# A 2x2x2 average pool: five 32 KB input buffers and a 32 KB first load in place of one 160 KB ring with a 64 KB first load

## The chip, the cores and the metric

The kernel runs on one core of a Trainium2 chip. Input and output lie in HBM, the chip's large memory; the work is done on tiles in SBUF, a memory of 128 partitions. The metric is the device time of one execution in microseconds (us). The kernel before takes 93.12 us, the median of three runs that lie between 93.12 and 93.19 us.

Three parts of the core matter here. SP (the sync engine) does no arithmetic: it issues every transfer of this kernel, one after the other, and can hold each issue back until a semaphore has a value. The 16 DMA engines carry the transfers. DVE (the vector engine) does all the additions. TensorE, ScalarE and, but for four constants that nothing here uses, GpSimd have no work.

## The reference

The input `x` is a float32 array of shape (8, 32, 32, 32, 32): batch, channels, depth, height, width. Every non-overlapping 2x2x2 block of depth, height and width is replaced by its mean:

```python
    out_d = d // kernel_size      # kernel_size is 2
    ...
    for i in range(out_d):
        for j in range(out_h):
            for k in range(out_w):
                ...
                window = x[:, :, d_s:d_s + kernel_size, h_s:h_s + kernel_size, w_s:w_s + kernel_size].copy()
                result[:, :, i, j, k] = np.mean(window, axis=(-3, -2, -1))
```

That is 33.55 MB to read and 4.19 MB to write, with seven additions and one multiplication for each output.

## The kernel before

Batch and channels together give 256 images, one to a partition: two tiles `t` of 128 partitions. An image is 32768 floats in a row, 128 KB. The kernel counts it in pieces of `KF` = 256 floats (1 KB): an image has 128 pieces, and 32 pieces are eight depth planes, 32 KB a partition, 4 MB over all partitions.

`plan` (line 42) lists the loads as (tile, first piece, pieces, place in the ring). The ring is a single SBUF tile of 160 pieces a partition. There are eight loads: one of 64 pieces (8 MB), five of 32 (4 MB) and at the end two of 16 (2 MB). The first four fill the ring exactly; the later four are written over parts that DVE has finished with.

`pool_unit` adds up what has landed, 32 pieces at a time or 16 for the two last loads, in place. Line 59 adds neighbouring depth planes, line 63 neighbouring columns, and line 66 neighbouring rows, multiplies by 0.125 and writes the result to one of two output tiles, `obuf`, one for each `t`. Line 66 also writes a sum to `dummy` that nobody reads; it shows in the profile as a short second instruction (DVE_READ_ACCUMULATOR2_ANT). Such a set of instructions is called a unit below: there are seven units of 32 pieces and two of 16.

Three stores on line 82 bring the results out: the whole first tile (2 MB, after the last unit of `t` = 0), 14/16 of the second (1.75 MB, after all its units but the last) and the last 2/16 (256 KB, after the last unit). They are written behind all loads in the program, and SP issues in the program's order: a transfer held back holds back all behind it. All transfers go through one hardware queue, in which each DMA engine takes its packets in order.

A framework derives the waits: a load into a part of the ring that was used before waits for the load that was there and for DVE's last instruction on it, a unit waits for its load, and a store for its units. At the end (line 92) SP waits for all transfers, two semaphores in one instruction, and all engines meet in a barrier. There is another barrier at the start, in a block ahead of the kernel's own. After compiling, the kernel takes the first load out of its own block and puts it into that opening block, ahead of SP's part of the barrier (its Drain instruction), so that the load leaves while the engines still meet. In the opening block as the kernel sees it at that point, SP's instructions begin with six that set registers (five moves and one that loads a base address); in the kernel before they stand ahead of the load.

Of the kernel before, what the change touches and what calls it, by code (L numbers as in the profile page):

```python
# [1 line left out]

# [4 lines left out]

F32 = mybir.dt.float32
KF = 256


@with_exitstack
def pool_rows(
    ctx: ExitStack,
    tc: tile.TileContext,
    x: bass.AP,
    kernel_size: int,
    out: bass.AP,
):
    nc = tc.nc  # L20
    assert kernel_size == 2, "only kernel_size == 2 supported"

    B, C, D, H, W = x.shape
    P = nc.NUM_PARTITIONS
    assert (B * C, D, H, W) == (2 * P, 32, 32, 32)
    add = mybir.AluOpType.add

    xv = x.rearrange("b c d h w -> (b c) (d h w)")  # L30
    ov = out.rearrange("b c d h w -> (b c) (d h w)")

    pool = ctx.enter_context(tc.tile_pool(name="ring", bufs=1))
    ring = pool.tile([P, 160 * KF], F32, name="ring")
    obuf = [pool.tile([P, 16 * KF], F32, name=f"obuf{t}") for t in range(2)]
    dummy = pool.tile([P, 1], F32, name="dummy")  # L40


    plan = [
        (0, 0, 64, 0),
        (0, 64, 32, 64),
        (0, 96, 32, 96),
        (1, 0, 32, 128),
        (1, 32, 32, 0),
        (1, 64, 32, 32),
        (1, 96, 16, 64),  # L50
        (1, 112, 16, 80),
    ]

    def pool_unit(buf, t, k0, kb):

        od = kb // 8
        a = buf.rearrange("p (o dd e) -> p o dd e", o=od, dd=2)
        b = buf[:, :od * 1024]
        nc.vector.tensor_add(  # L59
            out=b.rearrange("p (o e) -> p o e", o=od), in0=a[:, :, 0], in1=a[:, :, 1])  # L60
        bv = b.rearrange("p (e ww) -> p e ww", ww=2)
        c = buf[:, od * 1024:od * 1536]
        nc.vector.tensor_add(out=c, in0=bv[:, :, 0], in1=bv[:, :, 1])  # L63
        cv = c.rearrange("p (j hh k) -> p j hh k", hh=2, k=16)
        o0 = k0 * KF // 8
        nc.vector.tensor_tensor_reduce(  # L66
            out=obuf[t][:, o0:o0 + od * 256].rearrange("p (j k) -> p j k", k=16),
            in0=cv[:, :, 0], in1=cv[:, :, 1],
            scale=0.125, scalar=0.0, op0=add, op1=add, accum_out=dummy[:, :],
        )  # L70

    for t, k0, kb, r0 in plan:
        nc.sync.dma_start(
            out=ring[:, r0 * KF:(r0 + kb) * KF],
            in_=xv[t * P:(t + 1) * P, k0 * KF:(k0 + kb) * KF])
        for o in range(0, kb, 32):
            n = min(kb, 32)
            pool_unit(ring[:, (r0 + o) * KF:(r0 + o + n) * KF], t, k0 + o, n)


    for t, k0, kb in [(0, 0, 16), (1, 0, 14), (1, 14, 2)]:
        nc.sync.dma_start(
            out=ov[t * P:(t + 1) * P, k0 * KF:(k0 + kb) * KF],
            in_=obuf[t][:, k0 * KF:(k0 + kb) * KF],
        )


def kernel(tc: tile.TileContext, x: bass.AP, kernel_size: int, out: bass.AP):
    nc = tc.nc
    pool_rows(tc, x, kernel_size, out)  # L90
    tc.close()
    tc.compile()  # L92
    blocks = nc.main_func.blocks

    opening, program = blocks[0].instructions, blocks[tc.starting_block_idx].instructions
    load = next(i for i in program if isinstance(i, mybir.InstDMACopy))
    assert load.engine == nc.sync.engine
    barrier = next(  # L100
        n for n, i in enumerate(opening)
        if i.engine == load.engine and isinstance(i, mybir.InstDrain))
    program.remove(load)
    opening.insert(barrier, load)


# [1 line left out]
_INS = ['x', 'kernel_size']  # L108
_OUTS = [((8, 32, 16, 16, 16), 'float32')]

_NUMBERS = {'kernel_size': 2}


# [26 lines left out]
```

## Time and profile before

| what | value |
|---|---|
| median of three runs | 93.12 us |
| the profiled execution, its own time | 93.12 us |
| its span, first to last instruction | 91.3 us |
| DVE busy | 62.8 us, 69% of the span |
| DVE idle ahead of line 59, waiting for loads | 23.4 us, 22.0 us of it at the start |
| moved by DMA | 37.75 MB, mean 413 GB/s over the span |

The span begins with SP's first load at 0.00 us, and all times in the text count from there. 1.8 us of the execution's time lie outside of the span. A time "to landing" of a transfer counts from SP's issue until its last semaphore arrives, so issue and time to landing add up to the moment at which the data are there. SPq is SP's stream of issues and waits. The DMA share of a window counts each packet in the window in which it begins, so a short window can be well off; windows of several microseconds can be read.

### The profile page before, as it was taken

The page shows a single profiled execution, that of the slowest core. Times are in us where ns is not written, and L with a number is a line of the kernel's source. Part 1 is how long each engine was busy: PE and PEld are TensorE (multiplying, and loading weights), DVE is VectorE, ACT ScalarE, POOL GpSimd, SP SyncE. Part 2 cuts the span into 40 slices and gives each one's busy share as a digit, 9 for nine tenths or more (in the row PEclk, how much of TensorE's full clock was granted, in tenths as well). Part 3 has the DMA queues.
Part 4 walks back from the last instruction along what each step waited for, and adds up shares of the span by engine and source line. Part 5 has one row for each costly group of instructions (what it writes and reads, how often), then busy time and mean ns, then how long its engine had stood idle before and what let it go on. Part 6 is the DMA issues. An engine that isn't in the chain of part 4 may idle for free.

```text
span 91.3 us, 95 instructions
## 1 busy us (share of the span) xinstructions
DVE 62.8 (69%) x36; POOL 0.2 (0%) x4
## 2 busy tenths in 40 slices
DVE  0000000003999999999999999999993999999900
POOL 0000000000000000000000000000000000000000
DMA  9977799999999899999998899999997999899992
GB/s 459 430 344 344 316 402 459 459 459 459 445 402 416 373 430 459 459 459 459 445 402 387 387 445 459 459 459 459 416 416 337 438 431 445 309 423 445 410 413 109
DMA packets 1584, 37.75 MB, mean 413 GB/s; under 512 B 176, under 2 KB 176, under 8 KB 304
## 3 DMA queue, kind: packets, MB, share of 16 engines
q1 hardware_dynamic: 1584, 37.75, 97.4%
HBM read 33.55 MB, written 4.19 MB: 413 GB/s over the span
## 4 chain that ended last, share of the span: by engine, by line
DMA 55%; DVE 39%; issue 0%; DVEq 0%
DMA ring<-in_x_dram 55%; DVE ring L59 24%; DVE ring L63 10%; DVE obuf L66 5%; DVE dummy L66 0%; DVEq L92 0%
## 5 line engine op out<-in xcount | busy, mean ns | idle before, releaser
L59 DVE TENSOR_TENSOR ring<-ring 128x4096 f32<-128x4096 f32 (+1 forms) x9 | 35.4, 3946 | 23.4 <-DMA ring<-in_x_dram 23.4
L63 DVE TENSOR_TENSOR ring<-ring 128x2048 f32<-128x2048 f32 (+1 forms) x9 | 18.4, 2051 | 0.2
L66 DVE CUSTOM_DVE_ANT_1 obuf<-ring 128x1024 f32<-128x1024 f32 (+1 forms) x9 | 9.9, 1103 | 0.2
L66 DVE DVE_READ_ACCUMULATOR2_ANT dummy<- 128x1 f32 x9 | 0.7, 81 | 0.0
L121 POOL MEMSET const-uint8-127<- 128x1 uint8 x1 | 0.1, 103 | 0.0
L121 POOL MEMSET const-bfloat16-1.0<- 128x1 bf16 x1 | 0.1, 102 | 0.0
L121 POOL MEMSET const-float32-1.0<- 128x1 f32 x1 | 0.1, 99 | 0.0
L121 POOL MEMSET const-float32-0.0<- 128x1 f32 x1 | 0.1, 98 | 0.2 <-issue 0.2
## 6 DMA issues: line engine op xcount, KB each, us to landing
ring<-in_x_dram SPq DMA_DIRECT2D x5, 4096.0 KB, 30.8
ring<-in_x_dram SPq DMA_DIRECT2D x2, 2048.0 KB, 33.4
out_dram<-obuf SPq DMA_DIRECT2D x1, 2048.0 KB, 32.4
out_dram<-obuf SPq DMA_DIRECT2D x1, 1792.0 KB, 7.4
out_dram<-obuf SPq DMA_DIRECT2D x1, 256.0 KB, 3.8
ring<-in_x_dram SPq DMA_DIRECT2D x1, 21.9
```

Source lines behind the costliest of these rows:

```text
L59: nc.vector.tensor_add(out=b.rearrange("p (o e) -> p o e", o=od), in0=a[:, :, 0], in1=a[:, :, 1])
L63: nc.vector.tensor_add(out=c, in0=bv[:, :, 0], in1=bv[:, :, 1])
L66: nc.vector.tensor_tensor_reduce(out=obuf[t][:, o0:o0 + od * 256].rearrange("p (j k) -> p j k", k=16), in0=cv[:, :, 0], in1=cv[:, :, 1], s ...
L121: nc = _bacc.Bacc("TRN2", target_bir_lowering=False, num_devices=1)
```

## The change

The ring becomes a pool of five buffers of 32 pieces, of the same 160 KB together. The plan now lists eight buffers' contents, each loaded in one transfer of 32 pieces, or in two of 16 for the last two. So there are ten loads in place of eight: six of 32 pieces and four of 16. The former first load of 64 pieces is two loads of 32, and the load of `t` = 1 from piece 64 on, formerly 32 pieces, is two of 16. DVE does six units of 32 pieces and four of 16. The stores are the same three, with the same conditions. The first load is no longer put ahead of SP's Drain but ahead of SP's first instruction of the opening block.

```diff
-    pool = ctx.enter_context(tc.tile_pool(name="ring", bufs=1))
-    ring = pool.tile([P, 160 * KF], F32, name="ring")
-    obuf = [pool.tile([P, 16 * KF], F32, name=f"obuf{t}") for t in range(2)]
-    dummy = pool.tile([P, 1], F32, name="dummy")
+    pool_in = ctx.enter_context(tc.tile_pool(name="pin", bufs=5))
+    pool_out = ctx.enter_context(tc.tile_pool(name="pout", bufs=1))
+    obuf = [pool_out.tile([P, 16 * KF], F32, name=f"obuf{t}") for t in range(2)]
+    dummy = pool_out.tile([P, 1], F32, name="dummy")
...
     plan = [
-        (0, 0, 64, 0),
-        (0, 64, 32, 64),
-        (0, 96, 32, 96),
-        (1, 0, 32, 128),
-        (1, 32, 32, 0),
-        (1, 64, 32, 32),
-        (1, 96, 16, 64),
-        (1, 112, 16, 80),
+        (0, 0, (32,)),
+        (0, 32, (32,)),
+        (0, 64, (32,)),
+        (0, 96, (32,)),
+        (1, 0, (32,)),
+        (1, 32, (32,)),
+        (1, 64, (16, 16)),
+        (1, 96, (16, 16)),
     ]
...
-    for t, k0, kb, r0 in plan:
-        nc.sync.dma_start(
-            out=ring[:, r0 * KF:(r0 + kb) * KF],
-            in_=xv[t * P:(t + 1) * P, k0 * KF:(k0 + kb) * KF])
-        for o in range(0, kb, 32):
-            n = min(kb, 32)
-            pool_unit(ring[:, (r0 + o) * KF:(r0 + o + n) * KF], t, k0 + o, n)
+    for t, k0, parts in plan:
+        tin = pool_in.tile([P, 32 * KF], F32, tag="tin", name="tin")
+        views = []
+        o = 0
+        for kb in parts:
+            v = tin[:, o * KF:(o + kb) * KF]
+            nc.sync.dma_start(
+                out=v, in_=xv[t * P:(t + 1) * P, (k0 + o) * KF:(k0 + o + kb) * KF])
+            views.append((v, k0 + o, kb))
+            o += kb
+        for v, k, kb in views:
+            pool_unit(v, t, k, kb)
...
     load = next(i for i in program if isinstance(i, mybir.InstDMACopy))
-    assert load.engine == nc.sync.engine
-    barrier = next(
-        n for n, i in enumerate(opening)
-        if i.engine == load.engine and isinstance(i, mybir.InstDrain))
+    assert load.engine == nc.sync.engine and load.regs_accessed() == ((), ())
+    assert not load.sync_info.on_wait
+    first = next(n for n, i in enumerate(opening) if i.engine == load.engine)
     program.remove(load)
-    opening.insert(barrier, load)
+    opening.insert(first, load)
```

## The prediction

> **What bounds the kernel now.** I read the page first: busy shares, the slices with the DMA row, the chain that ended last, the groups.
>
> ```profile
> DVE 62.8 (69%) x36; POOL 0.2 (0%) x4
> ...
> DMA  9977799999999899999998899999997999899992
> ...
> HBM read 33.55 MB, written 4.19 MB: 413 GB/s over the span
> ...
> DMA 55%; DVE 39%; issue 0%; DVEq 0%
> ...
> L59 DVE TENSOR_TENSOR ring<-ring 128x4096 f32<-128x4096 f32 (+1 forms) x9 | 35.4, 3946 | 23.4 <-DMA ring<-in_x_dram 23.4
> ```
>
> The reader is to see two things that pull apart. The chain and the groups suggest that DVE matters: it idles 22 us for the 8 MB load, and its units make 39% of the chain. The DMA row says that the queue never rests. To tell which holds, I asked for the rate in stretches.
>
> ```profile
> 1.00:21.00 20.00, 0.00 (x0) 0.00 (x0) 1.00 1.01 419
> ...
> 30.70:40.40 9.70, 9.70 (x6) 0.00 (x0) 1.00 1.01 436
> ...
> 59.70:69.40 9.70, 9.20 (x7) 0.00 (x0) 1.00 1.00 432
> ...
> 77.00:80.30 3.30, 3.30 (x3) 0.00 (x0) 1.00 0.98 353
> ...
> 80.30:85.00 4.70, 4.63 (x7) 0.00 (x0) 1.00 1.01 431
> 85.00:88.90 3.90, 1.61 (x3) 0.00 (x0) 1.00 0.99 423
> ```
>
> The columns are the window, its length, DVE's and POOL's busy time, TensorE's clock, the DMA share and GB/s. From 1 us to the end of the stores the engines carry about 432 GB/s, with DVE busy or idle, reading or storing. The only dent is 77.0 to 80.3, where loads hand over to stores: 353 instead of 432 costs 3.3 x 79/432 = 0.6 us. Last, the issues at the end of the queue, with their time to landing:
>
> ```profile
> out_dram<-obuf SPq DMA_DIRECT2D x1, 2048.0 KB, 32.4
> ...
> out_dram<-obuf SPq DMA_DIRECT2D x1, 1792.0 KB, 7.4
> ...
> out_dram<-obuf SPq DMA_DIRECT2D x1, 256.0 KB, 3.8
> ```
>
> SP issues the three stores at 53.17, 82.48 and 86.68, so they land at 85.6, 89.9 and 90.5. The second is issued 3.1 us before the first has landed, the third 3.2 us before the second: both queue behind running work. So the bytes bound the kernel: about 1 us until the first packets, 37.75 MB without a gap, and 0.9 us from the last landing to the end of the span (90.5 to 91.3). DVE's share of the chain is work that runs into a full queue.
>
> **The change, part by part.** The profiled execution took 93.12 us, as the median did, so the sum is made against 93.12.
>
> *The first load ahead of six register instructions.* In the programs as they are built, neither has a register instruction on any engine; the first instruction of SP is the load in both, then its Drain. I take 0. Were they there, the nearest rows of SP are semaphore instructions of 17 ns, so 6 x 0.017 = 0.10 us, and the stretch from the end of the first issue (0.38) to the second (0.79), which holds Drain, semaphore and branch and 0.2 us of waiting: (0.41 - 0.2)/3 = 0.07 us each, 0.42 for six. Range -0.42 to 0.
>
> *The first load halved.* Loads of 32 pieces landed at 31.6 (0.79 + 30.8), 51.0, 60.8 (36.29 + 24.5) and 70.5 (41.77 + 28.7): 9.68 us each. The 64 pieces landed at 21.93, which is 2 x 9.68 plus 2.57 of start. If that start stays, the first half lands at 12.25 and the second at 21.93, and all behind it as before. DVE starts 9.7 us earlier and gains nothing by it, since nobody that DVE feeds is late: the first store goes out near 49 instead of 53.17, still far ahead of its turn. I take 0. The stretch from 1 to 21 us moves 419 instead of 432 GB/s, 0.6 us lost; half of it could go with packets of half the size, and an extra load's edge can cost at most what it costs below, 0.1. Range -0.3 to +0.1; I take 0, since the loss is in the start and not in the steady rows.
>
> *Load (1, 64) in two transfers of 16 pieces.* The two loads of 16 that are there:
>
> ```profile
> ring<-in_x_dram SPq DMA_DIRECT2D x1, 4096.0 KB, 28.7
> ...
> ring<-in_x_dram SPq DMA_DIRECT2D x1, 2048.0 KB, 31.4
> ...
> ring<-in_x_dram SPq DMA_DIRECT2D x1, 2048.0 KB, 35.4
> ```
>
> Issued at 41.77, 43.97 and 45.24, they land at 70.47, 75.37 and 80.64. The first half takes 4.90, so a pair like it takes 9.80 against 9.68 for the whole: +0.12. The other half takes 5.27, but that one has the dent. Bounds: 0 (a split is free) and 4.90 + 5.27 - 9.68 = +0.49. I take +0.12, by the half that is followed by another load, as both new ones are.
>
> The Trainium skill (DMA: Bandwidth & Descriptors, Anatomy of one DMA) fits one transfer as 2.0 us plus bytes at 436 GB/s. By that a 4 MB load would take 11.6 us and ten loads in a row 2 x 2.0 = 4.0 us more than eight, giving 97.1 us. The trace has 9.68 us between landings, so in a full queue that fixed part lies under the neighbour's bytes; the rule speaks of a lone transfer, and the sum here goes by the rows.
>
> *DVE's units.* The 32-piece unit takes 4.42 + 2.29 + 1.22 = 7.93 us, the 16-piece unit 2.29 + 1.22 + 0.69 = 4.20. One of the first becomes two of the second: +0.47 us of DVE, 64.4 us less overlaps. From the landings: the sixth unit runs 60.8 to 68.7, then 72.9, 77.1, 81.3 and 85.5 (the last load lands at 80.8 by then). So the second store is issued near 81.4 and the third near 85.6, about 1 us earlier than now, onto a queue that is busy until 85.7 and 90.0. Cost 0, covered by 4.3 us of queued bytes; even with DVE 3 us later it would still be covered.
>
> *Five buffers instead of the ring.* The sixth load waits for the first load and the first unit (12.25 + 7.93 = 20.2), the seventh and eighth for the second unit (29.9), the two behind for the third (39.3); they are due on the queue at 51, 60.8, 65.7, 70.6 and 75.5. Behind each waiting issue stand all later loads and stores, at least 31 us early. The fifth load now goes out at once instead of at 36.29. Cost 0.
>
> *The end.* SP waits for the transfers in four instructions of two semaphores. Before, the second of them holds the last store, and two follow its landing; the changed program has the last store's semaphore in the first, so three follow. One row more of 28 ns, by the estimate above 0.07 us with its dispatch. Bounds 0.03 and 0.1.
>
> ```profile
> L92 SPq EVENT_SEMAPHORE  x6: 17/28/3319, 87.1 to 91.3; - x6
> ```
>
> *The handover to the stores* is still the last load of 16 pieces against the same store: 0 change, bounds -0.6 (the dent goes) and +0.6 (it doubles).
>
> Sum: 0 + 0 + 0.12 + 0 + 0 + 0.07 + 0 = +0.19, so **93.31 us**. A difference of 0.2%, 0.186 us, is about what a measurement of this kernel can tell from none; the forecast lies on that edge, slower by a hair.
>
> **The rivals.**
>
> *The split is free.* DMA boundaries cost nothing, only the end's 0.07 remains, or not that: 93.12 to 93.19. For it: 423 to 432 GB/s across all kinds of boundaries. Against it: 4.90 twice is more than 9.68.
>
> *A faster start.* Place: the first packets, 1 to 4 us. If packets of 32 KB get through it 0.3 us sooner, or the load is really preceded by registers at present (up to 0.42 us), the time is 93.31 - 0.3 to 93.31 - 0.42, 92.9 to 93.0. It decides from 0.38 us on. For it: a load of half the packet size has never stood first in this trace. Against it: the built programs, and that a start-up delay need not shrink with the size.
>
> *The handover gets dearer.* Four loads of 16 pieces now lead up to the stores, and the first store is queued from 49 us on. If the dent of 0.6 us comes twice, 93.31 + 0.6 = 93.9. For it: 16-piece loads are the only ones near the dent. Against it: the first of the two ran at 4.90 and shows none.
>
> *DVE disturbs the loads.* DVE now works from 12 us, while the loads have that stretch to themselves before. Against it: 436 and 432 GB/s beside a full DVE. If the stretch 12 to 22 us lost 3%, 0.3 us, 93.6.
>
> **How the numbers follow.** The forecast's mechanism, a small loss by the split and the end, gets 0.52, with its own range 93.2 to 93.55; 0.32 of that lies above 93.31 and 0.20 below. The free split gets 0.14, the faster start 0.17, the dearer handover 0.13, DVE in the way 0.04. Slower: 0.32 + 0.13 + 0.04 = 0.49; same: 0.20 + 0.14 = 0.34; faster: 0.17. The range 92.85 to 93.75 holds the first three and the last case and, of the dearer handover, the part under +0.44; that leaves some 0.1 to 0.15 outside.
>
> **What would show it.** Right: the first load lands near 12.2 and the second near 21.9; DVE shows several idles ahead of line 58 instead of one large one; landings of later loads 9.7 us apart and of 16-piece loads 4.9; the stores land near 85.7, 90.0 and 90.6 in spite of being issued 1 us earlier; the span grows by about 0.2. Wrong: a second load that lands more than 0.3 us from 21.9 (start), a window of loads under 420 GB/s between 12 and 77 us, a handover of other than about 0.6 us, or a gap between the stores, which would mean that DVE's end matters after all.

## The result and the profile after

The changed kernel takes 93.49 us, the median of six runs between 93.35 and 93.71; the kernel before, run beside it, 93.20 us (93.12 to 93.29). The ratio is 1.0034 with a 95% interval of 1.0019 to 1.0049: slower by 0.29 us, where 0.19 was forecast. The one execution that was profiled is the longest of the six, 93.71 us with a span of 91.93, against 93.12 and 91.35 before; a part of what the two traces differ by is therefore chance, and the experiments below are needed to say which.

The page of the changed kernel, in the lines that answer to those shown of before:

```profile
DVE 64.1 (70%) x40; POOL 0.2 (0%) x4
...
DMA  8999889999999988999999987999999999999992
...
HBM read 33.55 MB, written 4.19 MB: 411 GB/s over the span
...
DMA 78%; DVE 13%; SPq 1%; issue 0%; DVEq 0%
...
L58 DVE TENSOR_TENSOR tin<-tin 128x4096 f32<-128x4096 f32 (+1 forms) x10 | 35.7, 3569 | 20.7 <-DMA tin<-in_x_dram 20.7
```

DVE's share of the chain fell from 39% to 13% and the time did not follow: DVE now works in step with the loads, and what it gave up on the chain was taken by DMA. The rate over the span is the same, 411 against 413 GB/s. The stretches and the issues, in the columns explained above:

```profile
1.00:21.00 20.00, 7.95 (x4) 0.00 (x0) 1.00 1.01 421
...
30.70:40.40 9.70, 7.95 (x4) 0.00 (x0) 1.00 1.00 432
...
59.70:69.40 9.70, 8.78 (x3) 0.00 (x0) 1.00 1.01 431
...
74.30:77.00 2.70, 2.63 (x5) 0.00 (x0) 1.00 0.98 407
77.00:80.30 3.30, 3.23 (x3) 0.00 (x0) 1.00 0.96 328
80.30:85.00 4.70, 4.45 (x5) 0.00 (x0) 1.00 1.02 436
85.00:88.90 3.90, 0.42 (x2) 0.00 (x0) 1.00 0.99 423
```

```profile
tin<-in_x_dram SPq DMA_DIRECT2D x1, 4096.0 KB, 12.0
...
tin<-in_x_dram SPq DMA_DIRECT2D x1, 4096.0 KB, 20.9
...
tin<-in_x_dram SPq DMA_DIRECT2D x1, 2048.0 KB, 40.2
...
tin<-in_x_dram SPq DMA_DIRECT2D x1, 2048.0 KB, 35.9
...
tin<-in_x_dram SPq DMA_DIRECT2D x1, 2048.0 KB, 41.2
...
out_dram<-obuf SPq DMA_DIRECT2D x1, 256.0 KB, 5.5
```

These were issued at 0.00, 0.79, 30.15, 39.48, 39.86 and 85.44. The trace also has each semaphore's own record, finer than the tenths in the rows; by it they land at 12.00, 21.70, 70.40, 75.41, 81.11 and 90.92. Against the same records of before: the first 64 pieces 0.23 us earlier (21.93 there), the pieces up to 96 of the second tile still 0.07 earlier (70.46), the next 16 pieces 0.05 later (75.36), the last load 0.44 later (80.68), the last store 0.50 later (90.43), the end of the span 0.59 later. So the start is shorter, the gain is gone before the stores, and another 0.1 us is lost behind the last landing. At the end, the row of SP's waits:

```profile
L96 SPq EVENT_SEMAPHORE  x6: 17/28/28, 90.9 to 91.9; - x6
```

The first of the four closing waits starts at 90.9 in this row, where it starts at 87.1 before. It holds the last store, and three more follow on it.

### The profile page after: what moved, and what is told of

Read it like the earlier page. It is cut to its first block, busy times and chain, and to the rows that moved or that the text cites. A ratio compares the mean times of both kernels' runs of the same rounds, so it can differ in the third digit from the quotient of the medians.

```text
span 91.9 us, 103 instructions
## 1 busy us (share of the span) xinstructions
DVE 64.1 (70%) x40; POOL 0.2 (0%) x4
## 4 chain that ended last, share of the span: by engine, by line
DMA 78%; DVE 13%; SPq 1%; issue 0%; DVEq 0%
DMA tin<-in_x_dram 78%; DVE tin L58 7%; DVE tin L62 4%; DVE obuf L65 2%; SPq L77 1%; DVE dummy L65 0%; DVEq L96 0%
## 5 line engine op out<-in xcount | busy, mean ns | idle before, releaser
L58 DVE TENSOR_TENSOR tin<-tin 128x4096 f32<-128x4096 f32 (+1 forms) x10 | 35.7, 3569 | 20.7 <-DMA tin<-in_x_dram 20.7
L62 DVE TENSOR_TENSOR tin<-tin 128x2048 f32<-128x2048 f32 (+1 forms) x10 | 18.6, 1864 | 0.3
L65 DVE CUSTOM_DVE_ANT_1 obuf<-tin 128x1024 f32<-128x1024 f32 (+1 forms) x10 | 10.1, 1010 | 0.3
```

The lines of the kernel that those rows point to most:

```text
L58: nc.vector.tensor_add(out=b.rearrange("p (o e) -> p o e", o=od), in0=a[:, :, 0], in1=a[:, :, 1])
L65: nc.vector.tensor_tensor_reduce(out=obuf[t][:, o0:o0 + od * 256].rearrange("p (j k) -> p j k", k=16), in0=cv[:, :, 0], in1=cv[:, :, 1], s ...
```

## The experiments

The theory after the result: the bytes bound both kernels, and the difference is small change at the edges of the queue: a start shorter by 0.23 us, a split that costs 0.1, waits at the end, and something dearer around the handover to the stores. Rivals for the last: DVE's early work beside the loads, the number of 16-piece loads, the depth of the queue, and 16 DMA engines that run closer in step. In each group the runs of the kernel before stand beside those of the experiments; its median was 93.28 to 93.31 us there.

**The first load halved, alone.**

```diff
-        (0, 0, 64, 0),
+        (0, 0, 32, 0),
+        (0, 32, 32, 32),
```

> The ring of before, with only its first load of 64 pieces made into two of 32 (nine loads, three stores). By the forecast's terms only the end's extra wait remains: before plus 0.07, near 93.27. If packets of half the size make the start 0.24 us shorter, as the landing of the second load in the changed kernel suggests (21.7 against 21.93), 93.2 - 0.24 + 0.07 = 93.0. If the loss near the handover comes from DVE running in step with the loads and the first store being queued 4 us earlier, it is here too: 93.0 + 0.4 = 93.4.

Measured: 93.47 us against 93.31, ratio 1.002 (1.0004 to 1.0036). The start is shorter here too: the second load lands at 0.78 + 20.9 = 21.7. And yet the median is 0.16 us above that of before, as much as in the second sample of the whole change below. That the halving itself costs this is not shown: with its twelve transfers the kernel also has the extra wait at the end, and two further kernels with a halved or quartered start, below, lie 0.07 and 0.09 above the kernel before.

**The split of load (1, 64), alone.**

```diff
-        (1, 64, 32, 32),
+        (1, 64, 16, 32),
+        (1, 80, 16, 48),
```

> The ring of before, with only the load of 32 pieces from (1, 64) on made into two of 16. By the forecast the split costs 0.12 and the end 0.07: 93.2 + 0.19 = 93.4. If four loads of 16 pieces ahead of the stores are what makes the last loads and the handover dearer by 0.4 us, 93.7 to 93.8, with the last load landing later than 80.64. If the loss comes from DVE in step instead, 93.3 to 93.4, since DVE starts late here as before.

Measured: 93.32 against 93.31, ratio 1.0001 (0.9988 to 1.0015). That is below the 93.4 of the forecast and far below the 93.7 of a dearer handover; it agrees with the 93.3 to 93.4 that was expected if DVE's step were the cause. In its trace the two halves take 9.79 us together (60.70 to 70.49, by the semaphores), where a whole load takes 9.71 in the trace of before, and the end has its extra wait, so both terms of the forecast are there; in the time they do not show. With four 16-piece loads ahead of the stores the handover is no dearer. Here is its stretch, and then that of the kernel before:

```profile
77.00:81.50 4.50, 4.43 (x7) 0.00 (x0) 1.00 0.98 368
```

```profile
77.00:81.50 4.50, 4.50 (x5) 0.00 (x0) 1.00 0.98 371
```

So the number of 16-piece loads falls as a rival.

**The first load in its old place.**

```diff
-    first = next(n for n, i in enumerate(opening) if i.engine == load.engine)
+    barrier = next(
+        n for n, i in enumerate(opening)
+        if i.engine == load.engine and isinstance(i, mybir.InstDrain))
     program.remove(load)
-    opening.insert(first, load)
+    opening.insert(barrier, load)
```

> The changed kernel, with the first load put ahead of SP's Drain as before. If the register instructions are not in the built program, this is the changed kernel again and shows how far two builds of one program lie apart: the changed kernel's 93.49, within 0.1. If six register instructions do stand ahead of the load here, 0.1 to 0.42 more: 93.6 to 93.9, with the other engines' first instructions earlier against the load.

Measured: 93.47 against 93.31, ratio 1.0016 (1.0001 to 1.0032); the runs lie between 93.11 and 93.73. SP's built program is the same, byte for byte, as that of the changed kernel. This is therefore a second sample of the change, +0.16 us beside the first sample's +0.29; its profiled execution took 93.24 us, 0.47 less than that of the changed kernel. That is what two profiles of one program can differ by.

**Three buffers.**

```diff
-    pool_in = ctx.enter_context(tc.tile_pool(name="pin", bufs=5))
+    pool_in = ctx.enter_context(tc.tile_pool(name="pin", bufs=3))
```

> The changed kernel with three buffers instead of five, so that loads are issued later (the last two near 59 us instead of 39.5) and fewer stand in the queue, the first store too. If a fuller or earlier queue is what slows packets from 40 us on, 93.49 - 0.3 = 93.2. If the depth is without effect, as the forecast has it, 93.5, and the queue still never runs empty.

Measured: 93.35 against 93.31, ratio 1.0008 (0.9994 to 1.0022). It lies between the two expected values, and its interval holds both the time of before and that of the changed kernel's second sample. Inconclusive in the time. In the trace the last loads go out near 59 us and the first store at 59.72, the queue never runs empty, and the dent is there as before (386 GB/s from 77.0 to 81.5).

**A light DVE.**

```diff
-        nc.vector.tensor_add(
-            out=b.rearrange("p (o e) -> p o e", o=od), in0=a[:, :, 0], in1=a[:, :, 1])
...
-        nc.vector.tensor_add(out=c, in0=bv[:, :, 0], in1=bv[:, :, 1])
```

> The changed kernel with the first two additions of each unit left out, so that DVE does only the last instruction (it adds rows of what was loaded, which is not the pool): 1.2 us a unit instead of 7.9, transfers as they are. If DVE's work beside the loads is what makes packets slow from 40 us on, the loads land evenly up to the handover and the time is that of the changed kernel without them, 93.5 - 0.2 = 93.25 or less. If the slow packets come from the 16 DMA engines standing closer in step after a start with half-size packets, they stay: 93.5.

Measured: 93.36 against 93.30, ratio 1.001 (0.9991 to 1.0029), with runs up to 93.82. The stretches of its trace decide more than the time:

```profile
60.00:77.00 17.00, 3.33 (x8) 0.00 (x0) 1.00 1.01 430
77.00:81.50 4.50, 0.51 (x1) 0.00 (x0) 1.00 1.01 371
```

DVE is busy for 0.51 us of the handover's 4.5, and the dent is as deep as in the kernel before, which has 371 in the same window beside 4.50 us of DVE (shown with the split alone). DVE's work does not make the dent. Nor does DVE bound the kernel: with a sixth of its work the time is that of before within the interval.

**DVE's second unit first.** The two first units were written in the other order, to make DVE begin at 21.4 us.

```diff
+    load(*plan[0])
+    load(*plan[1])
+    unit(*plan[1])
+    unit(*plan[0])
```

> The ring with its first load halved, as in the experiment on that alone, but DVE does the second unit first, so that it begins near 21.4 us as in the kernel before. If the early start of DVE is what costs, the shorter start remains as a gain and the extra wait at the end as a loss: 93.31 - 0.25 + 0.1 = 93.15. If it is the smaller packets at the start (engines closer in step), 93.47 as with the first load halved alone.

Measured: 93.37 against 93.30, ratio 1.0016 (1.0 to 1.0032). The framework's scheduler kept the first unit first, and DVE began at 12.12 us, so this did not test what it was made for. It stands as one more kernel with a halved first load, though not quite the same program as the first: the last instruction of the first unit comes behind the second instruction of the second unit, so the sixth load goes out at 31.13 us instead of 20.10.

**The first 64 pieces as 16, 16 and 32.**

```diff
-        (0, 0, 64, 0),
+        (0, 0, 16, 0),
+        (0, 16, 16, 16),
+        (0, 32, 32, 32),
```

> The ring with its first 64 pieces as loads of 16, 16 and 32. If the start shrinks with the packet (0.25 us from 64 KB to 32 KB), another 0.1 us: the first 64 pieces land near 21.2 instead of 21.34. DVE starts near 7 us. If an earlier DVE costs, the time is that of the first load halved, 93.47, or more; if the engines standing closer in step cost, more as well, 93.6; if neither does, 93.35.

Measured: 93.39 against 93.30, ratio 1.0007 (0.999 to 1.0023). The interval holds 93.35 as well as 93.47, and so decides between two of the expected values not at all; 93.6 lies outside. By the last packets, the DMA engines are through with the first 64 pieces at 21.32 us, against 21.57 before and 21.30 to 21.44 in the six traces so far that begin with 32 KB packets. Packets of 16 KB bring no more.

**The order of the waits at the end.** The closing Drain's list of waits was rebuilt with the last store's semaphore in the place that becomes the last of the four instructions. All waits are still there. Done to the kernel before, to the changed kernel and to the ring with a halved first load:

```diff
+    waits = list(end.sync_info.on_wait)
+    mine = next(w for w in waits if w.id == last)
+    waits.remove(mine)
+    waits.insert(1, mine)
```

> The kernel before with the order of SP's waits at the end changed, so that the last store's semaphore stands in the last of the four instructions instead of the second; nothing else moves. If each wait behind the last landing costs 0.065 us on the path, 0.13 less: 93.28 - 0.13 = 93.15, and from the last landing to the end of the span 1.11 us instead of 1.24. If the waits are hidden by something, 93.28.

> The changed kernel with the same edit: three waits no longer follow the last landing. 93.45 - 0.2 = 93.25, level with the kernel before, and 1.15 us from the last landing to the end instead of 1.36. If the end does not matter, 93.45.

> The ring with its first load halved and the same edit at the end: 93.43 - 0.2 = 93.23. If the shorter start is worth anything in the total, it shows here as a time below that of the kernel before with the same edit (93.15); if it is given back later, the time lies at or above it.

Measured against 93.28 for the kernel before: 93.18 (0.9993, 0.998 to 1.0006), 93.26 (1.0001, 0.9988 to 1.0014) and 93.17 (0.9988, 0.9973 to 1.0004). From the last packet of the last store to the end of the span the traces have 1.24 us before and 1.36 in the changed kernel; with the edit 1.13, 1.14 and 1.14. Counted from the last store's semaphore it is 0.92 us before, where two waits follow, 1.01 in the changed kernel, where three do, and 0.79 with the edit, in all three. The rows of the waits, of the kernel before and of the changed kernel, both with the edit:

```profile
L92 SPq EVENT_SEMAPHORE  x6: 17/28/3035, 87.0 to 91.3; - x6
```

```profile
L96 SPq EVENT_SEMAPHORE  x6: 17/28/302, 90.1 to 91.3; - x6
```

Against its own 93.47 the changed kernel has won some 0.2 us, as much as the stretch behind the last packet shrank in its trace (0.22). That it is now level with the unedited kernel before does not make the end the whole of the loss: the edit takes three waits out of the way, and the change had added one. The fair comparison is with the end alike in all three: the three medians lie within 0.09 us of one another, and the change's other parts sum to nothing that these runs can tell. The shorter start does not show in the total either, halved or not, 93.17 and 93.18; but each of these is good to about 0.13 us only, so a gain of 0.1 could hide there. The two fastest kernels of the study are these; both intervals still hold 1 against the kernel before.

**Engines closer in step.** A small load behind the first one, into a tile that nothing reads.

```diff
+        if r0 == 0 and t == 0:
+            nc.sync.dma_start(out=extra[:, :], in_=xv[0:8, 0:6 * KF])
```

> The kernel before with a small load of 8 rows of 6 KB behind the first one, into a tile that nothing reads. It goes to half of the DMA engines only. If that half is the one that runs ahead, the engines stand closer together afterwards (the spread of the first 64 pieces' last packets, 0.53 us before, falls to about 0.3). If a narrow spread is what makes later packets and the handover dearer, 93.28 + 0.08 (one more transfer, so one more wait behind the last landing) + 0.25 = 93.6. If the spread does not matter, 93.28 + 0.08 + at most 0.05 = 93.35 to 93.4.

Measured: 93.37 against 93.28, ratio 1.0013 (1.0001 to 1.0025), with all twelve runs between 93.29 and 93.47. The time is that of the indifferent case: the engines' packets behind the small load begin within 0.38 us of one another, against 0.53 before, and the time did not go to 93.6. But the trace holds more than was asked for, so this rival is weakened and not refuted: in it every engine's next packet after the small load takes about 0.39 us more than its like, those engines included that had no part in the small load, and the dent at the handover is missing. Here are the stretches of the kernel before with the last wait moved, as a yardstick, and then of this one:

```profile
20.00:24.00 4.00, 2.14 (x1) 0.00 (x0) 1.00 0.91 393
...
77.00:81.50 4.50, 4.50 (x5) 0.00 (x0) 1.00 1.02 386
```

```profile
20.00:24.00 4.00, 1.63 (x1) 0.00 (x0) 1.00 0.76 283
...
77.00:81.50 4.50, 4.50 (x5) 0.00 (x0) 1.00 1.00 426
```

**Two small loads,** the second behind the third load, with the last wait moved:

```diff
+        if (t, k0) in ((0, 0), (0, 96)):
+            e0 = 0 if k0 == 0 else 6 * KF
+            nc.sync.dma_start(out=extra[:, e0:e0 + 6 * KF], in_=xv[0:8, 0:6 * KF])
```

> The kernel before with the last store's wait in the last place, and with two small loads of 8 rows of 6 KB, one behind the first load as in the experiment on the narrow start and one behind the third, due on the queue near 41 us. There the first small load cost every DMA engine about 0.39 us at 21 us, and the dent at the handover to the stores was gone. If that is one loss which a queue takes once, wherever it is first disturbed, the second small load costs only its own packets, the handover shows no dent, and the time is 93.37 - 0.2 + 0.05 = 93.2. If each disturbance costs its 0.39 us by itself, 93.6. If the missing dent was a chance of one profile, the handover shows it again, and the time is 93.6 or more.

Measured: 94.09 against 93.28, ratio 1.01 (1.0077 to 1.0122).

```profile
20.00:24.00 4.00, 1.59 (x1) 0.00 (x0) 1.00 0.76 283
...
40.00:44.00 4.00, 3.97 (x2) 0.00 (x0) 1.00 1.01 365
...
77.00:81.50 4.50, 4.50 (x3) 0.00 (x0) 1.00 1.02 433
```

The dent is missing again, so that was no chance of one profile. But the second small load cost its own loss near 41 us, about 0.65 us by packet, and the two together some 0.9 us of time, 0.5 more than the 93.6 that was expected for a loss of 0.39 each time. One loss that a queue takes once is refuted; why the handover is smooth behind a small load stays open.

## Why the prediction was right

The forecast was 93.31, +0.19 us; the two samples of the change gave +0.29 (0.18 to 0.46) and +0.16 (0.01 to 0.30). The frame held: a queue that is full from 1 us to the end of the stores bounds both kernels, and DVE's ten earlier microseconds were worth nothing. That was read from the rate in stretches, against the chain of waits, which had put 39% on DVE; the light DVE confirms it.

The terms of the sum can be checked one by one, for twelve traces have no small load, and each part of the change is in some of them and not in others. The times go by the semaphores, in us:

| stretch | forecast | without the part | with it | difference |
|---|---|---|---|---|
| to the landing of the first 64 pieces | 0 | 21.84 to 21.93 (3 traces) | start halved or quartered: 21.65 to 21.80 (9) | about -0.16 |
| from there to the landing of the last load but one | +0.12 | 53.43 to 53.47 (5), 53.74 (1) | load (1, 64) split: 53.51 to 53.55 (5), 53.71 (1) | about +0.08 |
| from there to the landing of the last load | 0 | 5.32 to 5.58 (2) | any part: 5.37 to 5.73 (10) | scatter |
| from there to the landing of the last store | 0 | eight or nine loads: 9.74 to 9.77 (6) | ten loads: 9.81 to 9.83 (6) | +0.07 |
| from there to the end of the span | +0.07 | 0.92 (1) | three waits follow: 0.99 to 1.01 (8) | +0.07 to +0.10 |

The three closing kernels with the last wait moved are left out of the last row; they have 0.79. For the change the differences add up to about +0.08 us, and the last load scatters by 0.4 us. That sum lies in the interval of the second sample and below that of the first. That the forecast of +0.19 came so close to both is in part luck: it put at nothing a gain of 0.16 and a loss of 0.07, which partly cancel, and the runs are good to little better than 0.15. Point by point:

- *The register instructions*, 0: right, and shown. The old place gives the same program.
- *The first load halved*, 0 with bounds -0.3 to +0.1: right in the total as far as the runs can tell, but the reason, that the loss at the start would stay, was wrong. The start did shrink, by about 0.16 us. Alone, the halved load was 0.16 us slower than the kernel before; with the last store's wait moved as well, it was 0.11 faster (93.17 against 93.28).
- *The split*, +0.12: the right sign, a little too large. The prediction took 9.68 us for a whole load and 4.90 for a half, by issues and times to landing in tenths; by the semaphores of the same trace whole loads land 9.71 apart and the half takes 4.89, which gives +0.07. In the time of the kernel with the split alone it does not show, 1.0001, although that kernel also has the extra wait.
- *The end*, +0.07 with bounds 0.03 and 0.1: the mechanism right, and nearly the size. From the last semaphore the stretch grew by 0.09, from the last packet by 0.12, and moving the wait took away 0.22 in the changed kernel's trace and 0.11 in that of before. This is the one part of the change that an experiment shows to cost time.
- *DVE's units and the five buffers*, 0: nothing in the runs speaks against it. The second and third store went out at 80.98 and 85.44, 1.2 to 1.5 us earlier than before, onto a busy queue. No run has the ring with all ten loads, so the buffers alone were not tested.
- *The handover*, 0 within 0.6 either way: the dent cost about 0.8 us in the profile of the changed kernel (328 against 432 GB/s over 3.3 us) and 0.6 before. The last load is the widest term of the trace, and the runs do not tie it to the change. Nor is it shown to be a handover: the slow packets are those of the last load itself. Their usual 0.61 us goes up to 1.2 us between 77 and 79.6 us in the trace of before, and the first store's packets begin only at 79.8.
- *The signs of being wrong*: one came up. The changed kernel's trace has 407 GB/s from 74.3 to 77.0, under the 420 that was named. Its twin has 437 there, and the kernel before with the last wait moved 413, so a window this short does not tell the plans apart.

Of the rivals, the free split came nearest in the time of the split alone, though not in its trace; the faster start was real in its place, and in the total no run shows it. A dearer handover is not borne out: four 16-piece loads alone are as fast as before, and neither a first store that is queued only at 59.72 us nor a DVE with a sixth of its work takes the dent away. The fit of the Trainium skill (DMA: Bandwidth & Descriptors, Anatomy of one DMA — SWDGE (gpsimd) path), which the page gives for transfers issued from GpSimd, taken here as a price for every transfer in a row, would by estimate have given 97.1 us. Here SP issues them, one behind the other, and the measurement decides: two more loads in the full queue came to +0.16 and +0.29 us with all else that the change brought.

What stays open: why ten loads put 0.07 us between the last load and the last store, what makes the last load's packets slow, and what the first sample lost beyond the terms of the table. Its trace has slower packets in mid-run too (53.71 us in the second row), which that of its twin has not; with a spread of 0.4 to 0.7 us between runs of one kernel, twelve runs and one trace each do not settle it.

## What to carry to other kernels

Before crediting an engine's earlier start, look at the rate of the DMA queue in stretches: if it hardly dips, the chain of waits may run through the engine and still promise nothing. When two versions differ by a few tenths of a microsecond, read the ends: what follows the last landing is bare time, here 0.06 to 0.07 us for each closing wait behind the last store (0.79 us with none, 0.92 with two, 0.99 to 1.01 with three), and the order of those waits shifted with the number of transfers: with eleven the last store stood in the second of the four waits, with twelve and thirteen in the first. And profile a second build of the same program before explaining one trace: here two differed by 0.47 us.

## What was not expected

A load of 48 KB in a full queue was dearer than its bytes: at 432 GB/s they are 0.1 us, and on the engines that carried it its packet took 0.23 us; yet all 16 engines lost 0.39 us on their next packet in one place and about 0.65 in another, and two such loads made the kernel 0.9 us slower than its like without them (94.09 against 93.18). After such a load the dent near 78 us was gone (426 and 433 GB/s instead of 386), and with one small load the runs lay within 0.18 us of one another instead of 0.5. None of this was explained.
